# Residual block on one core: operand tiles at multiples of 128 bytes, w_out in 256-column halves, branch b in woven column pairs

## The chip, the cores and the metric

The kernel runs on one NeuronCore of a Trainium2 chip. The metric is the device time of one execution in microseconds (us); lower is better. A profile of one execution gives, for each engine, when each instruction ran and what it waited for. The engines are PE (TensorE: MATMUL, and its weight loads LDWEIGHTS, shown as PEld), DVE (VectorE), ACT (ScalarE), POOL (GpSimd) and SP (SyncE, which here only issues DMAs).

## The reference

One block of a network on x of 1024 rows (S) by 1024 columns (D), all in float32:

```python
h = rmsnorm(x, norm_mix_pre)
proj = h @ w_in                      # 1024 x 5128
q, k, v, f_logit, g_b, g_c, hc, gate_conv, gate_attn = split(proj)
ya = g_b * causal_depthwise_conv(g_c * hc, conv_w)        # 3 taps, 512 channels
yb = forgetting_attention(q, k, v, log_sigmoid(f_logit + b_f))  # 8 heads of 64
merged = sigmoid(gate_conv) * (ya @ w_branch[0]) + sigmoid(gate_attn) * (yb @ w_branch[1])
x = x + rmsnorm(merged @ w_out, norm_mix_post)
h = rmsnorm(x, norm_ffn_pre)
g, u = split(h @ w_gate_up)          # 2 x 2816 columns
x = x + rmsnorm((silu(g) * u) @ w_down, norm_ffn_post)
```

## The kernel before

Every product keeps float32's precision by splitting each operand into a high and a low part, both of type fp32r (`split`: ScalarE copies to hi, VectorE subtracts to get lo), and adding three matmuls, hi·hi, hi·lo and lo·hi (`mm3`). A matmul has a stationary operand of 128 x 128, which LDWEIGHTS brings in, and a moving operand of 128 x 512 mostly; its sum lies in one PSUM bank of 512 floats. The names hi, lo, hth, htl, hah, hal, hch, hcl, s4h, s4l, ghi, glo, woh, wol, yh, yl, wbh, wbl are all such halves of operands.

The large products (w_in, w_gate_up, w_down) run as Strassen-Winograd products, seven where eight would do the plain way; the sums of blocks that this needs (VectorE, GpSimd writes some to DRAM) run beside the matmuls. Their matmuls write to tiles named b (w_in, w_gate_up), ma and mb (the last pairs of w_in) and pd (w_down).

In time the stages are: the first norm, its transposes (tp) and the V and forget-gate projection (pv, 260 columns a matmul) up to 70 us; the products with w_in to 405; attention to 557, with scores sp, transposed probabilities tps, outputs po, and branch a's products (pba) as filler between them; the rest of branch a and then branch b (pbb) to 615; w_out (pm) with the norms and transposes around it to 710; the start of the FFN to 779; its first product to 1144; w_down to the end. Everything runs through one helper that records the instruction and, in stretches, holds it in program order, which is why all instructions carry one line, L75 before and L76 after the change. In the rest a scheduler orders each engine's instructions.

Places that the change touches:

- Pools and their tiles. Tiles lie one behind another in a pool, left or right side of SBUF, so the size of one sets where the next starts. `const` holds ident, tri, cw (the convolution's taps), bf and ff; `stat` small columns; `z` two tiles of 1024 + 2 floats, whose first two columns are zeros for the convolution; `a` and `av` the V projection's weights: raw in vf tiles, split in wvh and wvl, 520 columns read as two pieces of 260; `rsum` the attention's row sums; `gp` the last stage's tiles.
- Branch b multiplies 128 columns of w_branch[1] (wbh, wbl, stationary) by half of yb (yh and yl of `yb2`, moving, 512 columns) in 4 steps of k for each of 8 row blocks d and 2 halves n: 192 matmuls.
- `e_mm` multiplies 128 rows of the merged sum (mh, ml, stationary) by the 512 columns n of w_out (woh, wol), 8 steps of k, for 8 row tiles and 2 halves: 384 matmuls.

In the layout of the kernel before, the 512-column operands start at odd places: of 512 bytes, hth, hT12, hT34, hB11 and woh start at 32, hah, hch, hi, lo, s4h and s4l at 480, yh and yl at 352, ghi and glo at 160. The 260-column pieces of wvh and wvl start at 32, 48, 0 and 16 past a multiple of 64, in turns. ident starts at a multiple of 64.

Of the kernel before, what the change touches and what calls it, by code (L numbers as in the profile page):

```python
# [17 lines left out]
P = 128  # L18
# [16 lines left out]
C_GB, C_GC, C_HC = 1544, 2056, 2568  # L35
C_GATE_C, C_GATE_A = 3080, 4104
VF = AW + H
TAIL = 4
NPRE = 7

# [5 lines left out]
def block_kernel(  # L46
# [58 lines left out]
    def f32(ap):  # L105
        return ap.bitcast(F32)
# [10 lines left out]
    def copy(o, a):  # L117
        nc.scalar.activation(o, a, AF.Copy)
# [13 lines left out]

    cpool, _ = pool("const")
    stat, _ = pool("stat", 4, side="right")
    dpool, _ = pool("dram", space=DRAM)

    c_dram = dpool.tile([H, S], F32, name="c_dram")
# [9 lines left out]
    ri_dram = [dpool.tile([2, S], F32, name=f"ri_dram{j}") for j in range(4)]  # L147
    sg_dram = [dpool.tile([2, P, S], F32, name=f"sg_dram{d}") for d in range(8)]

    ident = cpool.tile([P, P], F32, name="ident")  # L150
    make_identity(bass_nc, ident)
    tri = cpool.tile([P, P], F32, name="tri")
# [1 line left out]
    ones = cpool.tile([P, P], F32, name="ones")  # L154
    nc.vector.memset(ones, 1.0)
    mask = cpool.tile([P, P], F32, name="mask")
    cw = cpool.tile([P, 3, 4], F32, name="cw")
    bf = cpool.tile([P, H], F32, name="bf")
    nc.gpsimd.dma_start(bf, b_f[0].partition_broadcast(P))
    ff = cpool.tile([P, ST, H], F32, name="ff")  # L160

    def bcast_row(row, p, **kw):
        g = p.tile([P, row.shape[-1]], F32, **kw)
# [27 lines left out]
    zp, z_close = pool("z", side="right")  # L191

    def z_tile(name, dt=F32, w=S):
        return zp.tile([P, S + 2], dt, tag="z", name=name, bufs=2)[:, :w]

    h_pool, h_close = pool("h1", side="right")
    def h_pair(name, shape):
# [6 lines left out]
    hB22 = h_pair("hB22", [P, 4, NC])  # L204
    ax, ax_close = pool("ax", side="right")
    ap, ap_close = pool("a")
    av, av_close = pool("av")
    psa, psa_close = pool("psa", 4, space=PSUM)

# [5 lines left out]
    wrs = []  # L215

    def vf_tile(tag="vf", dt=F32):
        return ap.tile([P, VF], dt, tag=tag, name=tag, bufs=6)

    def load_wv():  # L220
        k = len(wrs)
# [13 lines left out]
    xq.append(load_x(2))  # L235
    warm = st_tile("warm")
    nc.scalar.activation(warm, ones[:, 0:1], AF.Sqrt)
    wvh = av.tile([P, KT, VF], F32R, name="wvh")
    wvl = av.tile([P, KT, VF], F32R, name="wvl")
    gm = ax.tile([P, D], F32, name="gm")  # L240


# [12 lines left out]
    turns(14)  # L255

    def split_wv(k, halves="hl"):
        if "h" in halves:
            copy(wvh[:, k, :], wrs[k])
        if "l" in halves:  # L260
            sub(wvl[:, k, :], wrs[k], f32(wvh[:, k, :]))

    def norm_sum(st):

# [76 lines left out]

    def v_tile(st, ops):
        pv = psa.tile([P, 2, NC], F32, tag="pv", name="pv", bufs=2)
        hv = VF // 2
        for k in range(KT):
            src = ops[k // 4]
            for n in range(2):
                cs = slice(n * hv, (n + 1) * hv)
                mm3(
                    pv[:, n, :hv],  # L350
                    (src[0][:, k % 4, :], src[1][:, k % 4, :]),
                    (wvh[:, k, cs], wvl[:, k, cs]),
                    k == 0,
                    k == KT - 1,
                )
        vs = av.tile([P, VF], F32, tag="vs", name="vs", bufs=2)
        copy(vs.rearrange("p (n c) -> p n c", n=2), pv[:, :, :hv])
        nc.gpsimd.dma_start(v_dram[st * P : (st + 1) * P, :], vs[:, :AW])
        add(ff[:, st, :], vs[:, AW:VF], bf)

# [405 lines left out]
    def step_qk(t):  # L766
        j, rows_ = steps[t]
        if j not in rsums:
            rsums[j] = t0_.tile([P, 2 * ST], F32, tag="rsum", name="rsum", bufs=2)
        for i in rows_:  # L770
            sps[t, i] = qk(j, i)

# [53 lines left out]
    for ij, (kind, j, _, _) in enumerate(jobs):  # L826
# [28 lines left out]
        if kind == "qk":  # L855
            so = pp.tile([P, NC], F32, tag="so", name="so")
            copy(so, c11)
            for r, c, t in ((0, n1, so), (0, n2, c12), (1, n1, c21), (1, n2, c22)):
                nc.gpsimd.dma_start(qk_dram[j][r, :, c], t)
        elif kind == "z":  # L860
            zt = z_tile("zt", w=S + 2)
            nc.gpsimd.memset(zt[:, 0:2], 0.0)
            mul(zt[:, 2 : 2 + NC], c21, c11)
            mul(zt[:, 2 + NC : 2 + S], c12, c22)
            zts[j] = zt
        elif kind == "gb":
            for m, parts in ((j, (c11, c12)), (j + 1, (c21, c22))):
                zt = zts.pop(m)
                for n in range(2):
                    o = n * NC  # L870
                    ot = pp.tile([P, NC], F32, tag="so", name="ot")
                    nc.vector.tensor_scalar(
                        ot, zt[:, o + 2 : o + 2 + NC], cw[:, 2, m : m + 1], None, op0=ALU.mult
                    )
                    for t in (1, 0):
                        nc.vector.scalar_tensor_tensor(
                            ot, zt[:, o + t : o + t + NC], cw[:, t, m : m + 1], ot,
                            op0=ALU.mult, op1=ALU.add,
                        )
                    mul(ot, ot, parts[n])  # L880
                    nc.gpsimd.dma_start(ya_dram[m][:, o : o + NC], ot)
        else:
            so = c11
            strict[0] = ()
            if ij < len(jobs) - 1:
                so = pp.tile([P, NC], F32, tag="so", name="so")
                nc.scalar.activation(so, c11, AF.Sigmoid)
                for t in (c12, c21, c22):
                    nc.scalar.activation(t, t, AF.Sigmoid)
            for r, c, t in ((0, n1, so), (0, n2, c12), (1, n1, c21), (1, n2, c22)):  # L890
                nc.gpsimd.dma_start(sg_dram[j][r, :, c], t)
# [259 lines left out]
    for n in range(2):  # L1151
        nc.scalar.activation(sgs[KT - 1, n], sgs[KT - 1, n], AF.Sigmoid)
    m()
    yb2 = [halves_of(0)]
    for m in branch_a(KT - 2, 1, psm, "mm"):
        pass
# [15 lines left out]
    for n in range(2):  # L1172
        ns = slice(n * NC, (n + 1) * NC)
        for d in range(KT):
            ds_ = slice(d * P, (d + 1) * P)
            sg = sg_tile()
            nc.sync.dma_start(sg, sg_dram[d][1, :, ns])
            if d == KT - 1:
                nc.scalar.activation(sg, sg, AF.Sigmoid)
            ps = psm.tile([P, NC], F32, tag="mm", name="pbb")  # L1180
            for k in range(4):
                mm3(
                    ps, (wbh[k][:, ds_], wbl[k][:, ds_]),
                    (yb2[n][0][:, k, :], yb2[n][1][:, k, :]),
                    k == 0, k == 3,
                )
            mul(sg, sg, ps)
            add(um[:, d, ns], um[:, d, ns], sg)
            if n == 0:
                wr = flat(raw_t())  # L1190
                nc.sync.dma_start(wr, wout_d[d * P : (d + 1) * P, :])
                split(woh[:, d, :], wol[:, d, :], wr)
# [12 lines left out]
    def e_mm(st):  # L1205
# [4 lines left out]
        for n in range(2):  # L1210
            ns = slice(n * NC, (n + 1) * NC)
            ps = psm.tile([P, NC], F32, tag="mm", name="pm")
            for k in range(KT):
                mm3(
                    ps, (mh[:, k, :], ml[:, k, :]), (woh[:, k, ns], wol[:, k, ns]),
                    k == 0, k == KT - 1,
                )
            pm.append(ps)
        return pm

# [288 lines left out]
        return gp.tile([P, w], F32, name=name)  # L1509

    sums = {n: wide(f"sum_{n}") for n in ("c11", "c12", "c22", "c21", "both", "rest")}

    def sq_scale(o, c, key, sl):

# [100 lines left out]
```

## Time and profile before

| | us |
|---|---|
| median of 2 runs | 1361.85 (1361.17 to 1362.53) |
| the profiled execution's own span | 1362.4 |
| PE busy in it | 1341.2 (98%) |
| DVE busy | 933.0 (68%) |
| ACT busy | 535.5 (39%) |
| POOL busy | 128.0 (9%) |
| chain that ended last, share of PE work named b / pd / pm / pbb / pba | 28% / 16% / 5% / 3% / 2% |

Busy time counts an instruction from its start to its end with overlaps merged; a matmul of 512 columns is shown with a duration of some 390 ns while the next starts some 230 ns after it, so the distance from start to start, not the duration, is what a matmul costs. The chain of work is followed back from the last instruction, at each step to what released it; its pieces give a start, a length, and how many instructions of a kind followed one another. The profiled execution lies inside the range of the two runs.

### The profile page before, as it was taken

Reading aid. Unit: us, or ns where it says so; the run is one execution under the profiler, and the core shown is the slowest. Engines: PE = TensorE matmul, PEld = TensorE weight load, DVE = VectorE, ACT = ScalarE, POOL = GpSimd, SP = SyncE. Lnnn points to the kernel's source line nnn. Section 1 sums busy time; section 2 is a strip of 40 time slices with the busy share of each in tenths; the row PEclk is TensorE's granted clock in tenths of the full one; section 3 lists DMA queues with packets and bytes.
Section 4 is the critical chain, followed back from the end, with each engine's and each line's share of the span. In section 5 each row is a group of like instructions: output and inputs, shape, how many; then the busy total and the mean of one; then the engine's idle time right before and its main releaser. Section 6 shows DMA issues by size and latency. Waiting matters only on the chain.

```text
span 1362.4 us, 17714 instructions
## 1 busy us (share of the span) xinstructions
PE 1341.2 (98%) x6753; PEld 1099.8 (81%) x6753; DVE 933.0 (68%) x1445; ACT 535.5 (39%) x851; POOL 128.0 (9%) x256
## 2 busy tenths in 40 slices
PE   9999999999999999999999999999999999999997
PEld 7978888888887878788887788888888888888886
DVE  6974767754446766765668698676677766676585
ACT  6642222243345756514446232223222323444452
POOL 0001000010112212000002121100111011000000
PEclk9999999999999999999999999999999999999999
DMA  5432422333325545362235565322333236976441
GB/s 187 117 108 85 125 70 85 102 117 106 99 92 173 156 140 187 114 204 80 90 110 179 162 200 161 101 94 84 116 101 116 86 116 227 355 239 199 161 162 63
DMA packets 153256, 186.36 MB, mean 137 GB/s; under 512 B 9409, under 2 KB 106753, under 8 KB 153170
## 3 DMA queue, kind: packets, MB, share of 16 engines
q1 hardware_dynamic: 138434, 136.67, 32.5%
q0 software_dynamic: 14736, 48.54, 9.7%
q8 instruction: 53, 0.87, 0.3%
q14 instruction: 33, 0.27, 0.1%
HBM read 136.10 MB, written 49.09 MB: 136 GB/s over the span
## 4 chain that ended last, share of the span: by engine, by line
PE 58%; DVE 2%; issue 1%; DMA 1%; ACT 1%; POOL 0%; DVEq 0%; POOLq 0%; ACTq 0%
PE b L75 28%; PE pd L75 16%; PE pm L75 5%; PE pbb L75 3%; PE pba L75 2%; PE po L75 1%; PE tps L75 1%; PE sp L75 1%; DMA pre_dram<-s 1%; DVE tt L75 0%; DMA pre_dram<-c 0%; PE tp L75 0%; ACT tt L75 0%; DVE lo L75 0%; DMA raw<-in_w_gate_up_dram 0%
## 5 line engine op out<-in xcount | busy, mean ns | idle before, releaser
L75 DVE TENSOR_TENSOR c<-c,b 128x512 f32<-128x512 f32 x195 | 133.1, 683 | 93.2 <-PE b L75 68.3
L75 DVE TENSOR_TENSOR lo<-raw,hi 128x1024 fp32r<-128x1024 f32 (+1 forms) x93 | 112.1, 1205 | 86.0 <-PE b L75 71.5
L75 ACT ACTIVATE hi<-raw 128x1024 fp32r<-128x1024 f32 (+1 forms) x100 | 101.7, 1018 | 130.4 <-PE b L75 81.2
L75 PE MATMUL b<-hth,hi 128*128 128x512 f32 x352 | 139.1, 395 | 0.1
L75 PE MATMUL b<-hth,lo 128*128 128x512 f32 x352 | 138.1, 392 | 0.0
L75 PE MATMUL b<-htl,hi 128*128 128x512 f32 x352 | 137.2, 390 | 0.0
L75 ACT ACTIVATE hi<-sx 128x1024 fp32r<-128x1024 f32 x41 | 43.5, 1061 | 222.7 <-PE b L75 197.1
L75 PEld LDWEIGHTS b<-hth,lo 128*128 128x128 f32 x352 | 66.0, 188 | 15.6
L75 PEld LDWEIGHTS b<-hth,hi 128*128 128x128 f32 x352 | 66.1, 188 | 14.8 <-DVE c L75 1.0
L75 PEld LDWEIGHTS b<-htl,hi 128*128 128x128 f32 x352 | 66.1, 188 | 14.6
L75 DVE TENSOR_TENSOR lo<-sx,hi 128x1024 fp32r<-128x1024 f32 x41 | 50.2, 1225 | 34.6 <-PE b L75 30.8
L75 PE MATMUL b<-hah,hi 128*128 128x512 f32 x176 | 70.5, 403 | 2.1 <-ACT c L75 2.1
L75 DVE TENSOR_TENSOR sx<-raw 128x512 f32<-128x512 f32 x78 | 53.7, 688 | 23.4 <-DMA raw<-in_w_in_dram 11.7
L75 PE MATMUL b<-hah,lo 128*128 128x512 f32 x176 | 69.4, 395 | 0.0
L75 PE MATMUL b<-hal,hi 128*128 128x512 f32 x176 | 69.1, 393 | 0.0
L75 PE MATMUL pd<-hi,lo 128*128 128x512 f32 x160 | 62.6, 391 | 0.0
L75 PE MATMUL pd<-hi 128*128 128x512 f32 x160 | 62.3, 392 | 0.0
L75 PE MATMUL pd<-glo,ghi 128*128 128x512 f32 x148 | 57.7, 390 | 0.0
L75 PE MATMUL pd<-ghi 128*128 128x512 f32 x148 | 57.7, 390 | 0.0
L75 PE MATMUL pd<-ghi,glo 128*128 128x512 f32 x148 | 57.6, 389 | 0.0
L75 PE MATMUL b<-hT34h,lo 128*128 128x512 f32 x136 | 53.4, 393 | 0.0
L75 PE MATMUL b<-hT34h,hi 128*128 128x512 f32 x136 | 53.0, 390 | 0.4 <-DVE c L75 0.4
(369 smaller groups left out, 3367.8 us busy)
## 6 DMA issues: line engine op xcount, KB each, us to landing
raw<-in_w_gate_up_dram SPq DMA_DIRECT2D x51, 512.0 KB, 4.0
raw<-in_w_in_dram SPq DMA_DIRECT2D x35, 512.0 KB, 4.2
a_dramS<-um POOLq DMA_DIRECT2D x44, 256.0 KB, 3.1
a_dramA<-um POOLq DMA_DIRECT2D x33, 256.0 KB, 3.0
xt<-in_x_dram SPq DMA_DIRECT2D x16, 512.0 KB, 4.3
sg<-sg_dram SPq DMA_DIRECT2D x32, 256.0 KB, 4.1
graw<-a_dramS SPq DMA_DIRECT2D x14, 512.0 KB, 4.0
sg_dram<-c POOLq DMA_DIRECT2D x24, 256.0 KB, 2.3
```

Of the source, the lines that this page charges most:

```text
L75: ins = getattr(self.engine, name)(*args, **kw)
```

## The change

It has three parts. First, tiles are moved and padded so that every operand tile of a matmul starts at a multiple of 128 bytes: cw, bf and ff get a place ahead of ident and sizes that fill it, `stat`, `a` and `gp` get a pad, z tiles lose their two columns of zeros, vf and vs tiles and the two pieces of wvh and wvl are widened. Since z no longer has the zeros, the convolution's two steps with a tap further back leave out the first one or two columns of the first half instead, and four memsets go. Second, `e_mm` runs each of its matmuls as two of 256 columns, which write the two halves of the same PSUM tile. Third, branch b's matmuls read their moving columns and write their result in another order: columns 0, 1, 256, 257, 2, 3, 258, 259 and so on; both sides use the same order, so each value lands where it did.

```diff
...
 C_GB, C_GC, C_HC = 1544, 2056, 2568
 C_GATE_C, C_GATE_A = 3080, 4104
 VF = AW + H
+HV = VF // 2
 TAIL = 4
 NPRE = 7
 
...
 
     cpool, _ = pool("const")
     stat, _ = pool("stat", 4, side="right")
+    stat.tile([P, 24], F32, name="pad", bufs=1)
     dpool, _ = pool("dram", space=DRAM)
 
     c_dram = dpool.tile([H, S], F32, name="c_dram")
...
     ri_dram = [dpool.tile([2, S], F32, name=f"ri_dram{j}") for j in range(4)]
     sg_dram = [dpool.tile([2, P, S], F32, name=f"sg_dram{d}") for d in range(8)]
 
+    cw = cpool.tile([P, 4, 4], F32, name="cw")[:, :3, :]
+    bf = cpool.tile([P, 2 * H], F32, name="bf")[:, :H]
+    ff = cpool.tile([P, ST, H], F32, name="ff")
     ident = cpool.tile([P, P], F32, name="ident")
     make_identity(bass_nc, ident)
     tri = cpool.tile([P, P], F32, name="tri")
...
     ones = cpool.tile([P, P], F32, name="ones")
     nc.vector.memset(ones, 1.0)
     mask = cpool.tile([P, P], F32, name="mask")
-    cw = cpool.tile([P, 3, 4], F32, name="cw")
-    bf = cpool.tile([P, H], F32, name="bf")
     nc.gpsimd.dma_start(bf, b_f[0].partition_broadcast(P))
-    ff = cpool.tile([P, ST, H], F32, name="ff")
 
     def bcast_row(row, p, **kw):
         g = p.tile([P, row.shape[-1]], F32, **kw)
...
     zp, z_close = pool("z", side="right")
 
     def z_tile(name, dt=F32, w=S):
-        return zp.tile([P, S + 2], dt, tag="z", name=name, bufs=2)[:, :w]
+        return zp.tile([P, S], dt, tag="z", name=name, bufs=2)[:, :w]
 
     h_pool, h_close = pool("h1", side="right")
     def h_pair(name, shape):
...
     hB22 = h_pair("hB22", [P, 4, NC])
     ax, ax_close = pool("ax", side="right")
     ap, ap_close = pool("a")
+    ap.tile([P, 32], F32, name="pad")
     av, av_close = pool("av")
     psa, psa_close = pool("psa", 4, space=PSUM)
 
...
     wrs = []
 
     def vf_tile(tag="vf", dt=F32):
-        return ap.tile([P, VF], dt, tag=tag, name=tag, bufs=6)
+        return ap.tile([P, VF + 8], dt, tag=tag, name=tag, bufs=6)[:, :VF]
 
     def load_wv():
         k = len(wrs)
...
     xq.append(load_x(2))
     warm = st_tile("warm")
     nc.scalar.activation(warm, ones[:, 0:1], AF.Sqrt)
-    wvh = av.tile([P, KT, VF], F32R, name="wvh")
-    wvl = av.tile([P, KT, VF], F32R, name="wvl")
+    wvh, wvl = (
+        av.tile([P, KT, 2, HV + 12], F32R, name=n)[:, :, :, :HV] for n in ("wvh", "wvl")
+    )
     gm = ax.tile([P, D], F32, name="gm")
 
 
...
     turns(14)
 
     def split_wv(k, halves="hl"):
+        wr = wrs[k].rearrange("p (n c) -> p n c", n=2)
         if "h" in halves:
-            copy(wvh[:, k, :], wrs[k])
+            copy(wvh[:, k], wr)
         if "l" in halves:
-            sub(wvl[:, k, :], wrs[k], f32(wvh[:, k, :]))
+            sub(wvl[:, k], wr, f32(wvh[:, k]))
 
     def norm_sum(st):
 
...
 
     def v_tile(st, ops):
         pv = psa.tile([P, 2, NC], F32, tag="pv", name="pv", bufs=2)
-        hv = VF // 2
         for k in range(KT):
             src = ops[k // 4]
             for n in range(2):
-                cs = slice(n * hv, (n + 1) * hv)
                 mm3(
-                    pv[:, n, :hv],
+                    pv[:, n, :HV],
                     (src[0][:, k % 4, :], src[1][:, k % 4, :]),
-                    (wvh[:, k, cs], wvl[:, k, cs]),
+                    (wvh[:, k, n, :], wvl[:, k, n, :]),
                     k == 0,
                     k == KT - 1,
                 )
-        vs = av.tile([P, VF], F32, tag="vs", name="vs", bufs=2)
-        copy(vs.rearrange("p (n c) -> p n c", n=2), pv[:, :, :hv])
+        vs = av.tile([P, VF + 8], F32, tag="vs", name="vs", bufs=2)[:, :VF]
+        copy(vs.rearrange("p (n c) -> p n c", n=2), pv[:, :, :HV])
         nc.gpsimd.dma_start(v_dram[st * P : (st + 1) * P, :], vs[:, :AW])
         add(ff[:, st, :], vs[:, AW:VF], bf)
 
...
     def step_qk(t):
         j, rows_ = steps[t]
         if j not in rsums:
-            rsums[j] = t0_.tile([P, 2 * ST], F32, tag="rsum", name="rsum", bufs=2)
+            rsums[j] = t0_.tile([P, 4 * ST], F32, tag="rsum", name="rsum", bufs=2)[:, : 2 * ST]
         for i in rows_:
             sps[t, i] = qk(j, i)
 
...
             for r, c, t in ((0, n1, so), (0, n2, c12), (1, n1, c21), (1, n2, c22)):
                 nc.gpsimd.dma_start(qk_dram[j][r, :, c], t)
         elif kind == "z":
-            zt = z_tile("zt", w=S + 2)
-            nc.gpsimd.memset(zt[:, 0:2], 0.0)
-            mul(zt[:, 2 : 2 + NC], c21, c11)
-            mul(zt[:, 2 + NC : 2 + S], c12, c22)
+            zt = z_tile("zt")
+            mul(zt[:, n1], c21, c11)
+            mul(zt[:, n2], c12, c22)
             zts[j] = zt
         elif kind == "gb":
             for m, parts in ((j, (c11, c12)), (j + 1, (c21, c22))):
...
                     o = n * NC
                     ot = pp.tile([P, NC], F32, tag="so", name="ot")
                     nc.vector.tensor_scalar(
-                        ot, zt[:, o + 2 : o + 2 + NC], cw[:, 2, m : m + 1], None, op0=ALU.mult
+                        ot, zt[:, o : o + NC], cw[:, 2, m : m + 1], None, op0=ALU.mult
                     )
                     for t in (1, 0):
+                        back = 2 - t
+                        skip = 0 if n else back
                         nc.vector.scalar_tensor_tensor(
-                            ot, zt[:, o + t : o + t + NC], cw[:, t, m : m + 1], ot,
+                            ot[:, skip:], zt[:, o + skip - back : o + NC - back],
+                            cw[:, t, m : m + 1], ot[:, skip:],
                             op0=ALU.mult, op1=ALU.add,
                         )
                     mul(ot, ot, parts[n])
...
     for n in range(2):
         nc.scalar.activation(sgs[KT - 1, n], sgs[KT - 1, n], AF.Sigmoid)
     m()
+    def weave(t):
+        return t.rearrange("p (h i j) -> p i h j", h=2, j=2)
+
     yb2 = [halves_of(0)]
     for m in branch_a(KT - 2, 1, psm, "mm"):
         pass
...
             ps = psm.tile([P, NC], F32, tag="mm", name="pbb")
             for k in range(4):
                 mm3(
-                    ps, (wbh[k][:, ds_], wbl[k][:, ds_]),
-                    (yb2[n][0][:, k, :], yb2[n][1][:, k, :]),
+                    weave(ps), (wbh[k][:, ds_], wbl[k][:, ds_]),
+                    (weave(yb2[n][0][:, k, :]), weave(yb2[n][1][:, k, :])),
                     k == 0, k == 3,
                 )
             mul(sg, sg, ps)
...
             ns = slice(n * NC, (n + 1) * NC)
             ps = psm.tile([P, NC], F32, tag="mm", name="pm")
             for k in range(KT):
-                mm3(
-                    ps, (mh[:, k, :], ml[:, k, :]), (woh[:, k, ns], wol[:, k, ns]),
-                    k == 0, k == KT - 1,
-                )
+                for x, (a, b) in enumerate(((mh, woh), (mh, wol), (ml, woh))):
+                    for y in range(2):
+                        cs = slice(y * NC // 2, (y + 1) * NC // 2)
+                        nc.tensor.matmul(
+                            ps[:, cs], a[:, k, :], b[:, k, ns][:, cs],
+                            start=(k == 0 and x == 0 and y == 0),
+                            stop=(k == KT - 1 and x == 2),
+                            skip_group_check=True,
+                        )
             pm.append(ps)
         return pm
 
...
         return gp.tile([P, w], F32, name=name)
 
     sums = {n: wide(f"sum_{n}") for n in ("c11", "c12", "c22", "c21", "both", "rest")}
+    wide("pad", 80)
 
     def sq_scale(o, c, key, sl):
 
```

On the PE, at the end of branch b and the start of w_out (pbb is branch b's result, yh and yl its moving operand; pm is w_out's result, hi and lo the split merged sum), there stands before:

```order
L75 MATMUL pbb<-yh_5386,hi 128x512
L75 MATMUL pbb<-yl_5387,hi 128x512
L75 MATMUL pbb<-yh_5386,lo 128x512
L75 MATMUL pm<-woh,hi 128x512
L75 MATMUL pm<-wol,hi 128x512
L75 MATMUL pm<-woh,lo 128x512
```

and after the change:

```order
L76 MATMUL pbb<-yh_5384,hi 128x128x2x2
L76 MATMUL pbb<-yl_5385,hi 128x128x2x2
L76 MATMUL pbb<-yh_5384,lo 128x128x2x2
L76 MATMUL pm<-woh,hi 128x256 x2
L76 MATMUL pm<-wol,hi 128x256 x2
L76 MATMUL pm<-woh,lo 128x256 x2
```

The order is the same; the 192 matmuls of pbb have 128 groups of two pairs where they had 512 columns in a row, and each of pm's 384 is two of 256 columns one after the other. Every other matmul keeps its place and shape.

On GpSimd, at the end of the V projection (vs is V's result, so and c are results of w_in products on their way to DRAM), there stands before:

```order
L75 DMA bf<-in_b_f_dram 128x8
L75 DMA v_dram<-vs 128x512 x7
L75 MEMSET zt 128x2 x2
L75 DMA v_dram<-vs 128x512
L75 DMA qk_dram_66<-so 128x512
```

and after the change:

```order
L76 DMA bf<-in_b_f_dram 128x8
L76 DMA v_dram<-vs 128x512 x8
L76 DMA qk_dram_67<-so 128x512
L76 DMA qk_dram_68<-so 128x512
```

The memsets of the zero columns are gone, and nothing else on that queue has changed places.

## The prediction

> **What bounds the kernel now.** I read the page's busy line and its clock row first, then a table of stages, then the chain of work that ended last, then what the PE waited for.
>
> ```profile
> PE 1341.2 (98%) x6753; PEld 1099.8 (81%) x6753; DVE 933.0 (68%) x1445; ACT 535.5 (39%) x851; POOL 128.0 (9%) x256
> PEclk9999999999999999999999999999999999999999
> ```
>
> The PE is busy for 1341.2 of 1362.4 us and the granted clock stands in its top tenth in all forty slices. No other engine comes near. The stages (columns: stretch, length, then busy time and count of each engine, granted clock, DMA share, GB/s) say whether this holds everywhere:
>
> ```profile
> 70.00:405.00 335.00, 333.70 (x1459) 273.09 (x1458) 203.24 (x287) 104.63 (x132) 30.04 (x58) 1.00 0.33 98
> ...
> 557.00:615.00 58.00, 57.05 (x259) 46.36 (x260) 42.80 (x60) 20.54 (x27) 0.00 (x0) 1.00 0.54 169
> 615.00:710.00 95.00, 94.76 (x442) 77.62 (x441) 59.16 (x128) 40.23 (x87) 3.78 (x7) 1.00 0.29 100
> ...
> 779.00:1144.00 365.00, 364.55 (x1583) 297.12 (x1584) 270.08 (x378) 102.57 (x131) 42.93 (x79) 1.00 0.37 119
> 1144.00:1362.00 218.00, 211.58 (x926) 173.16 (x924) 150.23 (x184) 93.87 (x131) 2.72 (x5) 1.00 0.61 209
> ```
>
> These are the products with w_in (70 to 405), both branches (557 to 615), w_out (615 to 710), the FFN's first product (779 to 1144) and w_down. In each the PE works all but a few tenths or a few microseconds; the next engine, VectorE, has 74% at most. The longest pieces of the chain (start, length, what, count) are unbroken runs of matmuls:
>
> ```profile
> 559.52 11.15 PE pba L75 x48
> 570.68 44.50 PE pbb L75 x192
> ...
> 697.38 0.87 PE tp L75 x8
> 698.26 11.01 PE pm L75 x48
> ...
> 779.45 364.95 PE b L75 x1584
> 1144.40 211.20 PE pd L75 x924
> ```
>
> The waits for other engines are small; the two largest are
>
> ```profile
> PE b L75 <- ACT c L75: 3.0, 3, 2.1
> PE b L75 <- DVE c L75: 3.0, 3, 2.0
> ```
>
> So the time is a count of matmuls times the pitch from one start to the next. Those lengths give pitches of 364.95/1584 = 230.4 ns (b), 211.20/924 = 228.6 (pd), 11.01/48 = 229.4 (pm), 44.50/192 = 231.8 (pbb), 11.15/48 = 232.3 (pba), all for 512 columns: about 229.5 on average, or 0.448 ns per column. Anything that moves this pitch by 1 ns moves the kernel by some 4.8 us.
>
> **Is there room below 229.5?** Three kinds of matmul run beside the long ones. The transposes and their weight loads (duration minimum, median, maximum; first and last start):
>
> ```profile
> L75 PEld LDWEIGHTS tp<-ident,tt x64: 137/140/143, 636.8 to 737.1; 128*128 128x128 f32 x64
> ```
>
> Each has 128 columns and its own stationary block, and eight take 0.87 us: 108.8 ns each. That is nearly twice 128 x 0.448 = 57.3 ns, so I read it as two passes over 128 columns: 256 column steps at 0.425 ns, and no room left for a fixed cost. At that rate 512 columns take 217.6 ns, 11.9 less than now. The identity, which they stream, starts at a multiple of 64 bytes and is 512 bytes long. Every 512-column operand of the long runs starts 32 bytes past such a multiple (a few at other odd places); this is in the built program's addresses. The pitch does answer to addresses: in one stretch of pd
>
> ```profile
> 1174.58 0.39 PE L75 MATMUL pd<-ghi 128*128 128x512 f32 x1
> ...
> 1185.47 0.39 PE L75 MATMUL pd<-hi 128*128 128x512 f32 x1
> ```
>
> 48 matmuls, nearly all with both operands at 160 past a multiple of 512, take 10.89 us: 226.9 ns each, against pd's mean of 228.6. Against alignment speaks the V projection, whose 260-column matmuls start at offsets that go round 32, 48, 0 and 16:
>
> ```profile
> 66.07 0.28 PE L75 MATMUL pv<-wvh,hB22h 128*128 128x260 f32 x1
> ...
> 67.14 0.28 PE L75 MATMUL pv<-wvh,hB22h 128*128 128x260 f32 x1
> ```
>
> Nine in 1.07 us are 118.9 ns, 0.457 per column, and the three that start at 0 are no quicker. But a piece of 1040 bytes never ends on a whole block of 64, so this shows that an aligned start alone is not enough, not that whole blocks at both ends bring nothing.
>
> **Term 1, the operand tiles.** After the change every operand tile of a matmul starts at a multiple of 128 bytes. The matmuls of 512 columns outside w_out and branch b number 4476 (3276 b, 924 pd, 192 pba and 84 of the last products with w_in, ma and mb). Lower price: none, 0. Middle: the smoothest rows, 226.9, so 2.6 x 4476 = 11.6 us. Upper: the transposes' rate, 11.9 x 4476 = 53.3 us. I take the upper one, because only the transposes have what all matmuls get, whole blocks at both ends, and the pitch is known to depend on the address. The V projection and the attention's products are left at nothing; at 10 ns for each of 384 products the former would add 4 us.
>
> Nothing that the shorter pitch uncovers costs much. In 779 to 1144 VectorE has 270.08 us of work for some 346 us then; the last stage's DMA share of 0.61 would become 0.65.
>
> The Trainium skill, "TensorE: Matmul & The Clock Gate", section "Wait — 56ns, not 53.3ns?", gives back-to-back matmuls 215.7 ns for 512 columns; this case's trace has none that quick (226.9 at best), and by that page's figure term 1 would be 4476 x 13.8 = 61.8 us, an estimate.
>
> **Term 2, halves in w_out.** 384 matmuls of 512 columns become 768 of 256, each with a weight load of its own; before, these loads were hidden:
>
> ```profile
> L75 PEld LDWEIGHTS pm<-woh,hi x128: 187/188/190, 614.8 to 708.2; 128*128 128x128 f32 x128
> L75 PEld LDWEIGHTS pm<-wol,hi x128: 187/188/192, 615.0 to 708.4; 128*128 128x128 f32 x128
> ```
>
> Those two kinds have the same stationary block and load it twice already, so sharing saves nothing in the halves. Now 384 x 229.4 = 88.1 us; the stage is 94.76 of 95 us PE, so this lies on the path. Upper bound: 256 columns at pv's 0.457 are 117.0, x768 = 89.9, +1.8 us. Lower bound: the transposes' 108.8 (256 steps, own load), x768 = 83.6, -4.5 us. Is a weight load per 108.8 ns possible? The attention's products of 128 columns show loads at that pace:
>
> ```profile
> 472.58 0.28 PE L75 MATMUL sp<-lo,hi 64*128 64x256 f32 x2
> 472.69 0.28 PE L75 MATMUL sp<-hi,lo 64*128 64x256 f32 x2
> 472.81 0.22 PE L75 MATMUL sp<-hi 64*128 64x128 f32 x2
> 472.88 0.27 PE L75 MATMUL sp<-lo,hi 64*128 64x128 f32 x2
> 472.99 0.27 PE L75 MATMUL sp<-hi,lo 64*128 64x128 f32 x2
> ```
>
> Two with 256 columns start 0.11 to 0.12 us apart, and of 128 columns 0.07 and 0.11. I take -4.5, since it goes with term 1.
>
> **Term 3, woven pairs.** 192 pbb matmuls read and write two columns from one half, then two from the other, 1 KB apart: 256 pairs each, 49,152 in all, in a stage where the PE is busy for 57.05 of 58 us. No matmul of the trace has such a form. The nearest rows are VectorE's:
>
> ```profile
> L75 DVE COPY cs__1572<-cps 128x64 f32<-128x64 f32 x1 | 0.2, 218 | 0.0
> L75 DVE TENSOR_TENSOR s<-s 128x64 f32<-128x64 f32 x3 | 0.6, 202 | 0.1
> L75 DVE SCALAR_TENSOR_TENSOR s<-ff 128x64 f32<-128x64 f32 x1 | 0.2, 226 | 0.0
> ```
>
> The copy reads its 64 elements permuted and takes 218 ns, among 202 and 226 for unpermuted ones. Lower bound: it goes at term 1's pitch, 192 x 217.6 = 41.8, -2.7 us. Upper: a pair takes as long as a whole 32-byte piece, eight columns at 0.425 = 3.4 ns, 870 ns per matmul, 167.1 us in place of 44.5: +122.6. Between them, a pair as long as four columns: 435 ns, 83.6 us, +39.1. I take 0, by the permuted copy. VectorE reads the result as before, and its wait for pbb only follows.
>
> **What costs nothing.** Four memsets leave GpSimd, which has 0.00 us of work in 557 to 615 and 9% in all:
>
> ```profile
> L75 POOL MEMSET zt<- x4: 100/100/100, 64.9 to 212.2; 128x2 f32 x4
>   POOL zt L75: 24.3, 2
> ```
>
> The 24.3 us are GpSimd's own wait for z's buffer, behind which stood only its writes to DRAM; the chain has no such step. On SyncE's queue one load of attention's k moves down past three loads of w_in; it is issued at 233.6 us (of the two issues the first) and first used at 403.5, some 170 us later:
>
> ```profile
> L75 ACT ACTIVATE hi<-kl x3: 619/620/1065, 403.5 to 471.5; 128x512 fp32r<-128x512 f32 x2, 128x1024 fp32r<-128x1024 f32 x1
> L75 SPq DMA_DIRECT2D kl<-qk_dram x2: 339/362/385, 233.6 to 451.5; - x2
> ```
>
> Convolution steps of 510 or 511 elements instead of 512, and V's splits in two pieces of 260, lie under the PE's 333.70 of 335 us; without that cover they'd be under 1 us.
>
> **Sum.** Profiled execution 1362.4; -53.3 - 4.5 + 0 = 1304.6. The runs' median is 1361.85, 0.55 lower: **1304.0 us**, -4.2%. About 2% (27 us) is what a measurement of this kernel can tell from no change.
>
> **Rivals.**
>
> *Block rate (slower).* Streaming is served in pieces, and a pair of 8 bytes costs a piece. This is the same idea that makes alignment worth something, so the two go together. At 32 bytes: 1304.0 + 122.6 = 1426.6; without the alignment's gain it ends near 1486. It decides, to over 2% slower, from (1389.1 - 1304.0)/49,152 = 1.7 ns per pair, or from 0.5 ns if alignment brings nothing; half rate alone is 0.8 ns, so then 1363.7 + 39.1 = 1403. For it: the pitch knows addresses at all. Against: the permuted copy, which however takes 3 ns per element and could hide it. The Trainium skill, "Advanced Engine Details and Errata", section "Memory Cachelines", bears it out in part: "Any non-contiguous AP significantly slows down matmuls"; its next sentence asks only that every two consecutive elements be contiguous, which these pairs are. The Trainium skill, "Vector Engine (DVE) Microarchitecture Reference", section "5.2 Measured stream behaviour on trn2 (trn3 not measured)", has adjacent pairs at full rate with free hops between, for VectorE; no row here shows either for the PE.
>
> *Gain and half rate.* 1304.0 + 39.1 = 1343: within 2%.
>
> *Alignment does little.* The 11.9 ns per matmul belong to something else, such as the long row's change of weights; pv's aligned starts speak for it, the transposes, which change weights every time, against it. Then 1361.85 + 1.8 = 1363.7 with nothing gained, or 1352 with the smoothest rows' 2.6 ns: the layout doesn't do what it says.
>
> **Chances.** Forecast (whole gain, weaving free) 0.42, with a part of the gain but over 2% another 0.03; gain with half rate 0.11; little gain and free weaving 0.15; over 2% slower by weaving, with or without the gain, 0.29. Faster 0.45, same 0.26, slower 0.29. The range of 8 in 10 runs from 1291 (pv's and attention's products gain too, and pbb's 2.7) to 1420, which takes in half rate without gain and leaves out block rate and worse; the forecast's own range is 1291 to 1330.
>
> **What would show it.** Right: b at about 345 us for its 1584, pd about 201, pm about 10.4 per 96 halves, pbb 42 to 45 for 192, PE still over 97% busy. Wrong: pitches at 227 or above (term 1), pm over 11.1 per 96 (term 2), pbb over 47 us for 192 (term 3), or a chain where VectorE or DMA pieces of over 10 us stand between the runs of matmuls.

## The result: 1.1% slower, and the profile after

The changed kernel takes 1376.15 us (median of 2 runs, 1376.09 to 1376.21) against 1361.85 before: a ratio of 1.0106 with a 95% interval of 1.0087 to 1.0125. The forecast was 1304.0. The time lies inside the range given for 8 in 10 and among the cases "within 2%", but the forecast itself had the wrong sign. The interval is 0.2% to either side, far finer than the 2% that the prediction took for what a measurement can tell: the change does make the kernel slower.

The page's busy line and clock row show that nothing has changed in kind:

```profile
PE 1354.4 (99%) x7137; PEld 1121.5 (82%) x7137; DVE 933.1 (68%) x1445; ACT 535.6 (39%) x851; POOL 127.2 (9%) x252
PEclk9999999999999999999999999999999999999999
```

The PE still sets the time, at an undiminished clock, and has 13.2 us more of work. The waits for other engines are what they were (longest line 2.8 us instead of 3.0):

```profile
PE b L76 <- DVE c L76: 2.8, 3, 1.7
PE b L76 <- ACT c L76: 2.4, 3, 1.4
```

The chain's long pieces (start, length, what, count) give the new pitches:

```profile
556.83 10.89 PE pba L76 x48
567.73 65.27 PE pbb L76 x192
...
694.04 11.51 PE pm L76 x96
705.55 0.87 PE tp L76 x8
...
797.89 354.18 PE b L76 x1560
...
1163.93 203.68 PE pd L76 x896
```

b takes 354.18/1560 = 227.0 ns (230.4 before), pd 227.3 (228.6), pba 226.9 (232.3). A half of pm takes 119.9 ns, so two take 239.8 instead of 229.4. A woven pbb takes 340.0 ns instead of 231.8. So all three parts of the change moved the pitch, one down a little, two up. The signs of being wrong that the prediction had named are all there but the last: pitches at 227 or above (b and pd), pm over 11.1 us per 96 halves (11.51), pbb over 47 us (65.27); no long pieces of VectorE or of transfers stand between the runs of matmuls. Who waited for pbb shows that the woven products are the PE's own time and not a wait on the way:

```profile
L76 PE MATMUL pbb<-yl,hi x64: 509/513/514, 567.9 to 632.1; 128*128 128x512 f32 x64
...
L76 DVE TENSOR_TENSOR sg<-sg,pbb x16: 680/686/689, 571.8 to 633.2; 128x512 f32<-128x512 f32 x16
...
  PE pbb L76: 29.3, 15
```

VectorE's 16 products with pbb last 686 ns as before (682), but stood idle 29.3 us for pbb where it was 7.6. The transposes, 0.87 us for eight, did not change.

### The profile page after: what moved, and what is told of

Its sections match the earlier page's. It is cut to its first block, busy times and chain, and to the rows that moved or that the text cites. A ratio compares the mean times of both kernels' runs of the same rounds, so it can differ in the third digit from the quotient of the medians.

```text
span 1374.4 us, 18479 instructions
## 1 busy us (share of the span) xinstructions
PE 1354.4 (99%) x7137; PEld 1121.5 (82%) x7137; DVE 933.1 (68%) x1445; ACT 535.6 (39%) x851; POOL 127.2 (9%) x252
## 4 chain that ended last, share of the span: by engine, by line
PE 60%; DMA 2%; DVE 2%; issue 1%; POOL 0%; ACT 0%; SPq 0%; DVEq 0%; POOLq 0%; ACTq 0%
PE b L76 27%; PE pd L76 15%; PE pm L76 7%; PE pbb L76 5%; PE pba L76 2%; PE po L76 1%; PE tps L76 1%; PE sp L76 1%; DMA pre_dram<-s 1%; DMA tk<-in_w_down_dram 1%; PE tp L76 0%; DVE lo L76 0%; DMA pre_dram<-c 0%; DMA raw<-in_w_gate_up_dram 0%; DVE um L76 0%
## 5 line engine op out<-in xcount | busy, mean ns | idle before, releaser
L76 PE MATMUL b<-hT34l,hi 128*128 128x512 f32 x136 | 52.9, 389 | 0.0
```

The lines of the kernel that those rows point to most:

```text
L76: ins = getattr(self.engine, name)(*args, **kw)
```

## Experiments

### The three parts, one by one

Four kernels take the change apart; all ran on one chip, with a median of 1361.93 us for the kernel before beside them.

al_alone, the moved tiles only:

```diff
-                    weave(ps), (wbh[k][:, ds_], wbl[k][:, ds_]),
-                    (weave(yb2[n][0][:, k, :]), weave(yb2[n][1][:, k, :])),
+                    ps, (wbh[k][:, ds_], wbl[k][:, ds_]),
+                    (yb2[n][0][:, k, :], yb2[n][1][:, k, :]),
...
-                for x, (a, b) in enumerate(((mh, woh), (mh, wol), (ml, woh))):
-                    for y in range(2):
...
+                mm3(
+                    ps, (mh[:, k, :], ml[:, k, :]), (woh[:, k, ns], wol[:, k, ns]),
+                    k == 0, k == KT - 1,
+                )
```

> The changed kernel with w_out's matmuls at 512 columns again and branch b's columns in plain order, so the moved tiles alone. Theory (three prices that add up, read from the trace after: pitch 226.9 ns instead of 229.5 for 4476 + 576 matmuls, 120 ns per half, 340 ns per woven matmul): 1361.85 - 12 = about 1350 us, 0.9% faster, pm 227 and pbb 227 to 229 ns. Rival (the change's parts act on each other, and the smooth 226.9 of b and pd comes with the other two): 1358 or more.

1350.1 us, ratio 0.9913 (0.9899 to 0.9928). Its chain has

```profile
567.74 43.52 PE pbb L76 x192
...
772.06 354.23 PE b L76 x1560
```

pbb takes 226.7 ns, b 227.1. The tiles are worth 11.8 us. From start to start, without the waits (gaps of 300 ns and more), the matmuls of 512 columns have a mean of 229.45 ns in the kernel before and 227.05 here; 2.4 ns for 5052 of them are 12.1 us.

al_halves has only the first of these two edits (plain columns in branch b, halves in w_out).

> Moved tiles and halves in w_out, columns of branch b in plain order. Theory: each matmul carries a fixed 13 ns besides its columns, so 384 more of them cost 5 us: 1355, with pm at 120 ns per half and pbb at 227 to 229. Rival (the halves are slow because a stationary block comes in every 120 ns, which also disturbs what lies beside them): over 1358.

1354.11 us, ratio 0.9941 (0.9924 to 0.9958): 4.0 us more than al_alone.

al_weave has only the second (woven pairs, 512 columns in w_out).

> Moved tiles and woven pairs, w_out at 512 columns again. Theory: woven pairs cost 192 x (340 - 227) = 21.7 us: about 1371 us, pbb's 192 in 65.3 us, pm at 227 ns. Rival (pairs are slow only beside something else of the change): 1360 or less.

1372.01 us, ratio 1.0073 (1.0058 to 1.0089): 21.9 us more than al_alone. The three add up: 1361.9 - 11.8 + 4.0 + 21.9 = 1376.0, against 1376.15 measured.

old_weave is the kernel before with nothing but the woven columns of the diff.

> The kernel before with woven pairs in branch b and nothing else. Theory: the price belongs to the pattern, not to the addresses: 192 x (340 - 232) = 20.8 us more, 1382.6 us, pitch about 340 ns. Rival (the pairs collide because after the change both halves start at the same place of 512 bytes; here they start at 352 past it, but still 1 KB apart): a pitch under 300 ns, less than 1375 us.

1380.41 us, ratio 1.0137 (1.0122 to 1.0152). The chain of this run has

```profile
571.33 62.82 PE pbb L75 x192
```

327.2 ns each: the price belongs to the order of the columns and not to the new addresses, though on the new ones it is 13 ns larger.

### Which side of the woven matmul is slow

w_sides and w_runs give each of branch b's eight row blocks another order of columns; each ran once, and only distances inside the one execution are read. Where the order differs between read and write, VectorE's product reads PSUM and sg in the order that puts it right.

```diff
+            fr, fw = FORMS[d]
...
-                    weave(ps), (wbh[k][:, ds_], wbl[k][:, ds_]),
-                    (weave(yb2[n][0][:, k, :]), weave(yb2[n][1][:, k, :])),
+                    weave(ps, fw), (wbh[k][:, ds_], wbl[k][:, ds_]),
+                    (weave(yb2[n][0][:, k, :], fr), weave(yb2[n][1][:, k, :], fr)),
...
-            mul(sg, sg, ps)
+            mul(like(sg, fr, fw), like(sg, fr, fw), back(ps, fr, fw))
```

> Moved tiles, w_out at 512 columns; branch b's eight row blocks d differ in the order of columns (24 matmuls of each form): 0 plain; 1 pairs read and written; 2 pairs read, written plainly; 3 read plainly, pairs written; 4 runs of four columns read and written; 5 fours read only; 6 fours written only; 7 single columns from the two halves read only. Theory R (reading makes it slow): d=2 has 340 ns and d=3 227. Theory W (writing to PSUM does): d=2 227 and d=3 340. Each with a price per hop (113/256 = 0.44 ns): fours at 283 ns, singles at 453. Rival on the size of a line (16 bytes are one access): fours at 227.

Three pieces of the PE's timeline of w_sides (start us, duration us): pairs read only (d = 2, from 577 us), pairs written only (d = 3, from 580 us), singles read from the two halves (d = 7, from 590 us).

```profile
577.34 0.51 PE L76 MATMUL pbb<-yh,hi 128*128 128x512 f32 x1
577.67 0.51 PE L76 MATMUL pbb<-yl,hi 128*128 128x512 f32 x1
578.01 0.51 PE L76 MATMUL pbb<-yh,lo 128*128 128x512 f32 x1
...
580.43 0.39 PE L76 MATMUL pbb<-yh,hi 128*128 128x512 f32 x1
580.66 0.39 PE L76 MATMUL pbb<-yl,hi 128*128 128x512 f32 x1
580.89 0.39 PE L76 MATMUL pbb<-yh,lo 128*128 128x512 f32 x1
...
590.10 0.38 PE L76 MATMUL pbb<-yl,hi 128*128 128x512 f32 x1
590.32 0.38 PE L76 MATMUL pbb<-yh,lo 128*128 128x512 f32 x1
590.53 0.38 PE L76 MATMUL pbb<-yh,hi 128*128 128x512 f32 x1
```

The starts are 0.33 to 0.34, 0.23 and 0.21 to 0.22 us apart. Reading pairs is slow, writing them is free (theory R). The medians over 24 matmuls of each form, from the start of one to the start of the next:

| order of the moving columns | read and written | read only | written only |
|---|---|---|---|
| plain | 227 ns | | |
| pairs from two halves | 340 | 340 | 227 |
| fours | 251 | 250 | 231 |
| eights (w_runs) | 245 | 243.5 | 227 |
| sixteens (w_runs) | | 240 | |
| pairs from four quarters (w_runs) | | 443 | |
| pairs at a step of 16 bytes (w_runs) | | 451 | 227 |
| singles at a step of 8 bytes (w_runs) | | 451.5 | |
| singles from two halves | | **216** | |

> The same frame; by d: 0 runs of eight read and written; 1 eights read only; 2 eights written only; 3 sixteens read only; 4 pairs at a step of 16 bytes read (every other pair, then the rest); 5 pairs written at that step; 6 single columns at a step of 8 bytes read; 7 pairs read from four quarters in turn. If the price is per hop of the side found slow: eights 255, sixteens 241, d=7 and d=4 340. If it is per line: eights and sixteens 227, and a near hop may differ from a far one: d=4 below 340.

A price per hop (0.44 ns) would give 283, 255 and 241 for fours, eights and sixteens; 250, 243.5 and 240 were measured, and singles, which hop most, should have been at 453 and are the quickest of all. So neither theory of the price holds. The 231 ns of the written fours are no price of the write: in both halves n their first nine matmuls take 224 to 236 ns and the last three 226 or 227, and plain matmuls that follow another order settle in the same way. That single columns from the two halves in turn beat even the plain order by 11 ns was expected by none, and led to the next runs.

w_steps changes only the list of orders (`FORMS`), to singles at other steps.

> Branch b read in single columns at a step of S bytes, written plainly; by d: 0: S = 512 (four parts in turn), 1: 256, 2: 128, 3: 64, 4: 32, 5: 16, 6: 1024 (two halves in turn, 216 ns in the run before), 7: plain (227). Theory (two columns are fetched at once where they lie in different places, and one after the other where they lie close): 216 at 1024, 512 and some way down, 451 at the small steps as at 8 bytes. Rival (216 belongs to two places read in turn, as each line is used again at once): only d=6 is at 216, all others at 400 or more.

Two pieces of its timeline, singles at a step of 512 bytes (d = 0) and of 1024 (d = 6); in each piece the two rows are four matmuls apart:

```profile
568.02 0.45 PE L76 MATMUL pbb<-yh,hi 128*128 128x512 f32 x1
569.15 0.45 PE L76 MATMUL pbb<-yl,hi 128*128 128x512 f32 x1
...
598.25 0.38 PE L76 MATMUL pbb<-yh,hi 128*128 128x512 f32 x1
599.12 0.38 PE L76 MATMUL pbb<-yl,hi 128*128 128x512 f32 x1
```

1.13/4 = 283 ns at 512 bytes, 0.87/4 = 217.5 at 1024. The medians are 216 at 1024, 283 at 512, 487 at 256, 433 at 128 and 64, 431 at 32, 460 at 16. So 216 belongs to two places in turn, nearer to the rival; but the 283 of four places in turn lies between both expectations.

### What the fixed part of a matmul hangs on

cols cuts w_out's 512 columns differently in each of the eight row tiles:

```diff
+    COLS = [(512,), (256, 256), (128, 128, 128, 128), (384, 128), (320, 192), (448, 64), (512,), (256, 256)]
...
+                    if st in (6, 7):
+                        a, b = mb16, wb16
```

> Moved tiles, branch b plain; in w_out the eight row tiles st cut their 512 columns differently: 0: 512; 1: 256+256; 2: 4 x 128; 3: 384+128; 4: 320+192; 5: 448+64; 6: 512 and 7: 256+256 with operands in bfloat16 (these two tiles multiply other data: one block of 128 rows for all eight steps, so two row tiles of the output are not the reference's). Theory (13.3 ns per matmul besides 0.417 per column): 227, 120, 173 (384), 147 (320), 93 (192); below about 107 the weight load sets the pace instead (128 and 64). In bfloat16 the same 13.3 if it belongs to every matmul (227 and 120); rival: it belongs to the 4-byte operands, then about 216 and 109 as with the transposes' rate.

512 columns 227 ns, 256 columns 120, each 128 of four in a row 112; pairs of unequal pieces 286 (384 and 128), 257 (320 and 192), 313 (448 and 64). In bfloat16 512 columns take 216 and 256 take 109. So 4-byte operands in plain order have a fixed part of 2 x 120 - 227 = 13 ns per matmul, where the bfloat16 ones have 2 x 109 - 216 = 2 (nearer to the rival; these tiles also multiply one and the same block throughout, which was not tested by itself). A 4-byte piece of 128 or of 64 columns adds the same 112 to 113 ns whatever its columns: 384 and 128 are 13 + 160 + 112 = 285, and 448 and 64 are 13 + 187 + 113 = 313. That the weight load, the same for each piece, sets this floor fits, but was not shown apart. The fixed part is w_out's loss: 384 more of them would be 5.0 us; 4.0 were measured between al_halves and al_alone, and the rest of the difference is not explained.

narrow shortens the weight load: all but the first matmul of each sum take only the first M columns of the stationary block.

```diff
+    NARROW = [(128, None), (64, None), (32, None), (128, (2, 2)), (64, (2, 2)), (32, (2, 2)), (32, (4, 1)), (64, (128, 1))]
...
+                    m = P if k == 0 and x == 0 else M
...
+                        ps[:m], a[:, :m], b,
```

> Moved tiles; in w_out all matmuls of a row tile but the first of each sum use only the first M columns of the stationary block, so that its weight load reads M columns (the rest of the output rows then holds one of 24 products only). By st: plain reads with M = 128, 64, 32; pairs from the two halves with 128, 64, 32; then singles at a step of 512 bytes with M = 32 and at 16 bytes with 64. Theory (a plain read's 11 ns over the turned read's 216 is the weight load's reads in its way, 128 columns of it): 227, 221 to 222, 218 to 219, and pairs' 340 stays, as it is a matter of the moving read alone. Rival A (the 11 ns are the read's own): 227 at every M. Rival B (pairs too are slow through the weight load): 340, then well below 300 with 64 and 32.

Plain reads: 227 ns with M = 128, 230 with 64, 231 with 32. Pairs: 327 to 332, 328 mostly. The theory falls: a quarter of the weight load leaves the pitch where it was, so neither the 11 ns nor the price of pairs is a matter of its length. Singles at 512 bytes were at 275 in one half and 283 in the other, and at 16 bytes at 460, much as in w_steps.

### What the placing of tiles does

sh_all and sh_left take al_alone and move tiles by 32 bytes again:

```diff
-    bf = cpool.tile([P, 2 * H], F32, name="bf")[:, :H]
+    bf = cpool.tile([P, H], F32, name="bf")[:, :H]
...
-    stat.tile([P, 24], F32, name="pad", bufs=1)
+    stat.tile([P, 32], F32, name="pad", bufs=1)
```

Both edits are in sh_all, only the first is in sh_left.

> Moved tiles alone, and then every tile on both sides of SBUF 32 bytes lower (bf's place in const 32 bytes smaller, stat's pad 32 larger), so that all operands start at 480 past a multiple of 512. Theory P (what counts is that the two operands of matmuls that follow each other have the same place within 512 bytes): pitch 227, about 1350 us. Rival A (what counts is a start on a whole block of 64 or 128 bytes): pitch 229.5 or more again, about 1362 us.

1350.31 us, ratio 0.9908 (0.9891 to 0.9924), the same as al_alone's 1350.1, though no operand of the large products starts on a multiple of 64 any more. What the change's pads are made for, a start at a multiple of 128 bytes, is not what brings the gain.

> Moved tiles alone, and then only the tiles on the left side of SBUF 32 bytes lower (480 past a multiple of 512), those on the right side at 0. All stationary operands of the large products lie left; the moving ones lie left (w_down's pd, hah, hal, hch, hcl) or right (hth, htl, hT12, hT34, hB, woh, wol). Theory P (the two operands' places within 512 bytes must agree): pd stays at 227 ns, b with hth or hT and pm go to about 229 to 231, together 2900 matmuls x 2 to 3 ns = 6 to 9 us more than 1350. Rival A (what counts is that each operand, or one side alone, starts on a whole block): pd at 229.5 too, or nothing changes where both differ.

1370.56 us, ratio 1.0058 (1.0041 to 1.0075), 20 us above al_alone and slower than the kernel before. Its chain has w_out (pm) and most of b, with the moving operand right and the stationary one left, and w_down (pd), with both left:

```profile
704.97 11.21 PE pm L76 x48
...
768.92 383.39 PE b L76 x1644
...
1158.73 203.68 PE pd L76 x896
```

pm takes 11.21/48 = 233.5 ns, b 383.39/1644 = 233.2, pd 227.3. Among the b's, those with the moving operand right (hth, htl, hT12 and so on) have a mean of 233 to 234. This is theory P, with over twice the price expected (6 to 7 ns, not 2 to 3).

Not all of it fits: hah with hi has both operands at 480 and still a mean of 233.0 here and 233.5 before the change. The same shows when the starts of a trace are sorted by the addresses in the built program (means of matmuls followed by one with the same places, gaps of 270 ns and more left out):

| run | moving, stationary (past a multiple of 512) | matmuls | ns |
|---|---|---|---|
| al_alone | 0, 0 | 4971 | 227.0 |
| sh_all | 480, 480 | 4971 | 226.9 |
| sh_left | 480, 480 | 1957 | 228.1 |
| sh_left | 0, 480 | 2848 | 233.4 |
| kernel before | 160, 160 | 431 | 227.3 |
| kernel before | 480, 480 | 1044 | 229.9 |
| kernel before | 32, 480 | 2844 | 229.2 |
| kernel before | 352, 480 | 314 | 231.9 |

In the kernel before, two operands at the same 480 were no quicker than two at 32 and 480. So the runs show that one place for all tiles gives 227 ns; which tiles have to agree they don't show. Nor do they show that the measure is 512 bytes: all places of the kernel before are equal within 64, and 352 and 480 within 128, and neither brought 227; places equal within 256 alone were not tried.

### Turned reads everywhere

turn_all marks the PSUM tiles of b, pd, pm, pba and pbb, 4968 of the 5052 matmuls of 512 columns. (Its list names ma and mb too, but these tiles are made where nothing is marked; their 84 matmuls keep the plain order and 227 ns.) A matmul into such a tile reads its moving columns from the two halves in turn, and whoever reads it does so at a step of two columns:

```diff
+                if name == "matmul" and id(args[0]) in woven:
+                    args = (args[0], args[1], args[2].rearrange("p (h i) -> p i h", h=TURN))
+                elif name != "matmul" and any(id(a) in woven for a in args):
+                    args = [
+                        a.rearrange("p (i h) -> p h i", h=TURN) if id(a) in woven
+                        else a.rearrange("p (h i) -> p h i", h=TURN)
+                        if tuple(getattr(a, "shape", ())) == (P, NC) else a
+                        for a in args
+                    ]
```

> Moved tiles, and every matmul of 512 columns reads its moving columns one by one from the two halves in turn and writes plainly; VectorE and ScalarE read the sums at a step of two columns, which puts them in order again. Theory (the 216 ns of the turned reads holds everywhere): 5050 x 11 ns = 55 us less than 1350, about 1295 us, if reading PSUM at a step costs VectorE and ScalarE nothing (VectorE's product with pbb took 687 ns so, 680 plainly). Rival (the longer stages differ, or the other engines' 290 reads of PSUM become slow and hold the PE up): 1320 or more.

1304.6 us, ratio 0.9579 (0.9565 to 0.9594): the best of all versions, 4.2% below the kernel before and 5.2% below the change. Its chain:

```profile
539.16 10.36 PE pba L93 x48
549.52 41.44 PE pbb L93 x192
...
791.44 300.86 PE b L93 x1392
1104.52 194.24 PE pd L93 x896
```

215.8, 215.8, 216.1 and 216.8 ns. VectorE pays nothing for the step of two; its commonest group, of al_alone and then of turn_all:

```profile
L76 DVE TENSOR_TENSOR c<-c,b x195: 675/681/689, 84.5 to 1131.8; 128x512 f32<-128x512 f32 x195
```

```profile
L93 DVE TENSOR_TENSOR c<-c,b x195: 674/680/690, 83.6 to 1097.6; 128x512 f32<-128x512 f32 x195
```

Of the expected 55 us, 45.5 came, against al_alone. The pitches are as expected; the PE's idle time, the span less its busy time, is 1305.6 - 1279.8 = 25.8 us in the page's line:

```profile
PE 1279.8 (98%) x6753; PEld 1107.6 (85%) x6753; DVE 930.3 (71%) x1445; ACT 534.5 (41%) x851; POOL 127.5 (10%) x252
```

In al_alone it was 20.1 (1349.1 - 1329.0). So 5.7 us of the gain turned into idle time, and the PE's work fell by 49.2 us. Most of the remaining difference is waits as well: a matmul is shown with 379 ns and the next starts after 216, so a pause of up to some 160 ns does not show as idle. All that the distances from start to start have above the pitch (227 ns in al_alone, 216 here) adds up to 7.3 us among the b's of al_alone and 15.7 here, for pm to 1.5 and 3.6, for pd to 0.8 and 1.7: 11.4 us more, besides 0.9 us for the 84 matmuls in plain order. That is all of the shortfall to within 2 us.

old_turn has the same turned reads in the kernel before, with its own tiles.

> The kernel before, with its own layout and without the change, but with the moving columns of all 512-column matmuls read one by one from the two halves in turn, as in turn_all. Theory (the time over 216 ns in a plain read comes from the moving operand meeting the weight load's reads in the same places; a read that turns between two places meets it less, so the layout no longer counts): 216 to 218 ns, 1300 to 1315 us. Rival (turned reads still need both operands at the same place within 512 bytes): 220 ns or more on average, over 1320 us, with some 20 us between this and turn_all.

1304.28 us, ratio 0.9579 (0.9563 to 0.9595). The chain has

```profile
549.59 41.44 PE pbb L92 x192
...
788.33 300.86 PE b L92 x1392
1101.03 194.24 PE pd L92 x896
```

to the hundredth what turn_all has. With turned reads the layout no longer counts. The result is as this theory had it; its reason, a meeting with the weight load, found no support in narrow, where a load of a quarter of the columns did not shorten the pitch.

## Why the prediction was wrong, point by point

**What bounds the kernel** held: the PE, by count times pitch, in every stage, and no other engine or transfer came to the fore. The edits costed at nothing cost nothing: al_alone, which has all of them, gained 11.8 us where its pitches alone make 12.1. One figure is off without harm: a nanosecond of the pitch is worth 5.05 us (4476 + 384 + 192 matmuls), not 4.8.

**Term 1 was mis-sized**: 53.3 us taken, 11.8 measured, of which the 4476 matmuls of the term make about 10 us (2.3 ns each, from start to start) and w_out and branch b the rest. Its middle price, 2.6 ns or 11.6 us, was close. The row behind it, 226.9 ns in w_down's smooth stretch, was a good witness partly by luck: its operands share one place, 160 past a multiple of 512, but matmuls of the same trace with both operands at 480 had a mean of 229.9. The step that failed was to take the transposes' 0.425 ns per column for what any aligned matmul gets. They stayed at 108.8 ns when all tiles moved, and the 512-column matmuls did not come near. The V projection's rows, where an aligned start brought nothing, were the better witness, and were argued away; with all its pieces at multiples of 64 after the change, a matmul of 260 columns still took 120 ns in the median, as before. The Trainium skill, "TensorE: Matmul & The Clock Gate", section "Wait — 56ns, not 53.3ns?", has 215.7 ns for 512 columns back to back; after the change the trace had 227, and runs with bfloat16 operands or turned reads had 216. So the figure holds on this chip, but not for a plain read of 4-byte columns.

**The mechanism of term 1 was wrong too.** Blocks at both ends have nothing to do with it: with every tile 32 bytes off the gain stayed, with one side off it turned into a loss.

**Term 2 was mis-sized**: -4.5 us taken, +4.0 measured, beyond the upper bound of 1.8. The step that failed was to take the lower bound, the transposes' 108.8 ns, for a half of w_out: it took 119.9. The upper bound used the V projection's 118.9 ns per 260 columns as a price per column; in cols each matmul has a fixed part of some 13 ns, which halving pays twice.

**Term 3 was mis-sized**: 0 taken, 20.8 us by the pitch, 21.9 by the run. The bounds (-2.7 to 122.6) held it. The step that failed was to take VectorE's permuted copy for the PE's read: the PE needs 340 ns where the pairs are read and 227 where they are only written. The Trainium skill, "Advanced Engine Details and Errata", section "Memory Cachelines", has that any non-contiguous pattern slows matmuls, and asks for pairs to be contiguous; it says so of PSUM, where here pairs, fours and eights were written at no price worth naming (227 to 231 ns). The price was on the side of the read.

**The chances.** The outcome is a mixture of two rivals: alignment does little (1352) and a price for woven pairs of about half of "half rate" (20.8 us where that has 39.1). Little gain with half rate was there, at 1403; a price of pairs between nothing and half rate was not. All three terms erred in the same direction, by 41.5, 8.5 and some 21 us. That the time still lies in the range of 8 in 10 is the width of the range and not the merit of its working.

**What stays open.** Why a plain read of 4-byte columns takes 11 ns more than one from two halves in turn, and why pairs in turn cost 113 ns more, is not shown. The runs exclude the write, the length of the weight load and starts on whole blocks. Which tiles have to share a place, and what the equal places act on, was not found either.

## What to carry to other kernels

A pitch that is quicker in one corner of a trace is a price for other instructions only where engine, form and order agree; here neither the transposes nor a copy on VectorE stood for a long matmul. When a kernel is bound by the count of matmuls, a test of a few read orders in one stage (one row block each, in one run) costs little: it found 11 ns per matmul, four times what the careful placing of tiles brought. If tiles are placed, give all of them the same place within 512 bytes; moving one side alone cost 20 us here.

## What the runs showed of the hardware that I had not expected

- A matmul of 512 fp32r columns started every 216 ns when its moving columns were read one by one from two halves 1 KB apart, every 227 ns in plain order, every 340 ns in pairs from these halves, and every 431 to 487 ns in singles at steps of 256 bytes and less.
- VectorE read PSUM at a step of two columns in 680 ns per 512, as in plain order (681).
- With the tiles of one side of SBUF moved by 32 bytes (sh_left), matmuls whose operands lie on different sides took 233.4 ns, 6 to 7 more than with all tiles at 0; all tiles at 480 past a multiple of 512 were as good as all at 0 (226.9 and 227.0 ns).
- With reads in turn the place no longer counted: 215.8 ns for pbb in turn_all and in old_turn.
